# Moving elementwise work from GpSimd to VectorE, and reordering the convolution stage, in a two-layer hybrid trunk

## The chip, the cores and the metric

The kernel runs on one core of one Trainium2 chip, in one launch. The metric is the device time of one execution in microseconds. The engines are named as in the profile: PE is TensorE's matmul, PEld its weight load, DVE is VectorE, ACT is ScalarE, POOL is GpSimd and SP is SyncE, which issues most of the transfers. L508 is line 508 of the kernel's file.

## The reference

Two layers of a diffusion trunk run over 128 context tokens and 512 latent tokens with a width of 1024. Cut to what matters here:

```
mod = ada_w-projection of silu(condition)             # 6 vectors a layer: shift, scale, gate (twice)
h   = rmsnorm(x) * norm_w * (1 + scale) + shift
# layer 0
p   = h @ ab_w_in                  # DeltaNet q, k, v, gate z, a, b; attention q, k, v
qkv = silu(depthwise_conv5(dq, dk, dv));  dq, dk = l2norm(dq), l2norm(dk)
o_dn = rmsnorm(delta_forward(...) + delta_backward(...)) * silu(z)     # chunkwise, a triangular inverse a chunk
o_at = attention(rope(rmsnorm(aq)), rope(rmsnorm(ak)), av)
x   = x + gate * (concat(o_dn, o_at) @ ab_w_out);  x = x + gate * swiglu(adaln_norm(x))
# layer 1: the same frame with a bidirectional mLSTM as the mixer
```

All of it is float32. A product is made of three passes over two-part operands: each operand is split into a rounded part `hi` (fp32r) and the remainder `lo = x - hi`, and the products are hi·hi, lo·hi and hi·lo.

## The kernel before

Activations lie transposed, as 8 tiles of 128 features by 640 tokens. Weights come in a fixed order (`wspecs`); `WStream.fetch` loads a unit on the SP queue, casts `hi` on ScalarE (L483) and subtracts `lo` (L484) on the engine held in `W.eng`, up to three units ahead of the product that uses them. SBUF is handed out from 30 slots in the order in which they were freed. The framework orders each engine's instructions by program order and readiness; each engine then runs its own queue strictly in turn.

The stages that the change touches, in order:

- **Start** (`ada_start`). For each of 8 feature tiles: a scale vector from two VectorE reductions over a weight tile, then `nm.scale` (hi and lo of the scaled x) and `nm.square` (running sum of squares), and products of the first 272 output columns. For odd tiles lo and the running sum are made on GpSimd.
- **Convolutions** (`conv`, 12 feature tiles of k, q, v). A product of 48 matmuls (`qkv`), an evacuation to `cbuf`, one ScalarE and four VectorE taps (`cy`, L980), then a queue `later` of closures. `tick()` runs one closure after each product. The closure of tile n does its SiLU (L984), some modulation pieces (`ada_fill`, two VectorE reductions of 1024 columns, L323), and `then()`: five transposes on TensorE (`flip`, L992 and L994) and what follows them. So the transposes of tile n stand behind the product of tile n+1. The first two tiles use the scaled, not yet normalized x (`nm.raw`, the norm is applied in the evacuation as `cu`), while `nm.finish` makes the normalized `h` for the others.
- **Gate, attention queries and keys** (`gemm_tok` with `ev_z`, `ev_q`, `ev_kv`). Modulation pieces are attached to the evacuations: `ADA_CONV` gives 9 pieces to the convolutions, `ADA_Z` and `ADA_Q` 5 each, `ADA_KV` none. In `ev_q` the piece comes before the norm and rope of the tile.
- **Decay matrices** (L1157 to L1168): 40 VectorE products `up`, which read PSUM, followed by attention, and beside attention a triangular inversion on GpSimd (L1218, L1220) and then the DeltaNet scan.
- **Output projection of layer 0** (`out_half`, 16 units of 24 matmuls). Each unit is added into x by VectorE (`resid`, L558); in the second half the scale and the sum of squares of the next norm follow. The weight remainders and the sums of squares are GpSimd's.
- **Head of layer 1.** Four products with raw x, `nm.finish`, and then the token-major products. The weight remainders, and the scaling of the first two query tiles, are GpSimd's.

GpSimd has the powers for every reciprocal square root (`rsqrt`, L154) and its own DMA queue too.

Of the kernel before, what the change touches and what calls it, by code (L numbers as in the profile page):

```python
# [53 lines left out]
ADA_CONV, ADA_Z, ADA_Q, ADA_KV = [1] * 9 + [0] * 3, [1] * 5, [1] * 5, [0, 0, 0, 0, 0]  # L54
# [31 lines left out]
def tile_trunk(ctx: ExitStack, tc: tile.TileContext, A, dbg=None, stop=None):  # L86
# [101 lines left out]
    class Norm:  # L188
# [24 lines left out]
        def scale(self, k, x, eng=dve):  # L213
            h, sc = self.raw, self.sc
            v = None if eng is dve else t_tile("nv")[:, :T]
            for s, (a, b) in enumerate(SEG):
                act.activation((h.hi[k] if v is None else v)[:, a:b], x[:, a:b], AF.Copy, scale=sc(s, k))  # L217
                if v is None:
                    dve.scalar_tensor_tensor(out=h.lo[k][:, a:b], in0=x[:, a:b], scalar=sc(s, k),
                                             in1=h.hi[k][:, a:b].bitcast(F32), op0=ALU.mult, op1=ALU.subtract)  # L220
# [4 lines left out]
        def add(self, k, x, eng=dve):  # L225
            if self.raw:
                self.scale(k, x)
            self.square(k, x, eng)

        def square(self, k, x, eng=dve):  # L230
# [126 lines left out]
    def ada_start(nm):  # L357
# [15 lines left out]
        def x_in(k):  # L373
            sp.dma_start(out=xs[k], in_=A["x"][k])
            nm.square(k, xs[k], pool if k in (1, 3, 5, 7) else dve)
# [16 lines left out]
        def products(k):  # L392
# [3 lines left out]
            for t in range(NT):  # L396
# [6 lines left out]
              "s": lambda k: nm.scale(k, xs[k], pool if k in (1, 3, 5, 7) else dve)}  # L403
# [61 lines left out]
    class WStream:  # L465
        def __init__(self):
            self.i = 0
            self.eng = dve
# [92 lines left out]
    def out_half(mx, xs, l, half, nm, js=range(NK), fill=0, eng=dve, spill=None):  # L561

        for j in js:
            w = W.next(3)
            ps = g_tile("op")
            gemm_f(ps, w, mx, 4 * half, 4)
            U.put(*w[2])
            resid(ps, xs[j], mod[l][2], j)
            ada_fill(fill[j] if fill else 0, xs[j][:, 0:1])
            if nm is not None:  # L570
                nm.add(j, xs[j], eng)
            if spill is not None:
                pool.dma_start(out=spill[j], in_=xs[j])
# [285 lines left out]
    def layer0(nm, accs, ws, xt, xs):  # L859
        with ExitStack() as lay:  # L860
# [73 lines left out]
            def bias_b():  # L934
                for s in range(2):
                    pb = m_tile("shb")
                    pe.matmul(pb[:, :272], lhsT=ident[0:2, s:s + 1].to_broadcast([2, P]), rhs=shr[0:2, :272],
                              start=True, stop=True)
                    act.copy(shw[:, 272 * s:272 * s + 272], pb[:, :272])
                for t, n, b in ((slice(0, 1), 1, 0), (slice(1, NT), NT - 1, 272)):  # L940
                    pool.tensor_tensor(out=gat[:, t, :], in0=gat[:, t, :],
                                       in1=shw[:, None, b:b + 16].to_broadcast([P, n, 16]), op=ALU.add)
                    pool.tensor_tensor(out=zv[0][:, t, :], in0=zv[0][:, t, :],
                                       in1=shw[:, None, b + 16:b + 272].to_broadcast([P, n, 256]), op=ALU.add)
                act.activation(zv[0], zv[0], AF.Silu)
                gates_a()
# [13 lines left out]
            def conv(ft, x, out, then):  # L960
# [13 lines left out]
                tick()  # L974
# [28 lines left out]
            def after_k(hh):  # L1003
# [8 lines left out]
                if hh == 3:  # L1012
                    dve.tensor_scalar(out=ssk, in0=ssk, scalar1=EPS, scalar2=None, op0=ALU.add)
                    rsqrt(rk, ssk)
                    pool.tensor_tensor(out=nk, in0=ssk, in1=rk, op=ALU.mult)
                    pool.tensor_tensor(out=rk2, in0=rk, in1=rk, op=ALU.mult)
                    for d in range(2):
                        pool.tensor_tensor(out=bU[:, :, 4 * d:4 * d + 4], in0=beta[:, :, 4 * d:4 * d + 4], in1=rk2, op=ALU.mult)
                    pool.tensor_tensor(out=sK, in0=sK, in1=bU, op=ALU.mult)

            def after_q(hh):
                p0, p1 = flip(kq[hh][:, 648:1296])
                sumsq(ssq, hh, p0, p1)
                if hh == 3:
                    dve.tensor_scalar(out=ssq, in0=ssq, scalar1=EPS, scalar2=None, op0=ALU.add)
                    rsqrt(rq, ssq)
                    pool.tensor_scalar(out=rq, in0=rq, scalar1=128.0 ** -0.5, scalar2=None, op0=ALU.mult)
                    pool.tensor_tensor(out=rq2, in0=rq, in1=rq, op=ALU.mult)

            rk = sm([NT, 4], "rk")  # L1030
            W.eng = pool
# [4 lines left out]
            for hh in range(4):  # L1036
# [5 lines left out]
                if hh == 1:  # L1042
# [21 lines left out]
            W.eng = dve  # L1064
# [59 lines left out]
            def ev_kv(t, ps):  # L1124
                raw = t_tile("ak")
                act.copy(raw[:, :256], ps[:, 0:256])
                ada_fill(ADA_KV[t], raw[:, 0:1])
                act.copy(vav[:, t], v3(ps[:, 256:512], 2))
                n = norm_rope(t, raw, 2, kw)
                if t == 0:  # L1130
# [285 lines left out]
            def finish(c):  # L1416
# [9 lines left out]
                pool.tensor_tensor(out=rs, in0=rs, in1=rq[:, c, :], op=ALU.mult)  # L1426
# [58 lines left out]
    def layer1(nm, xt, xs, xd):  # L1485
        with ExitStack() as lay:
# [23 lines left out]
            W.eng = pool  # L1510
# [7 lines left out]
            for j in range(4):  # L1518
# [3 lines left out]
                (pool if j < 2 else dve).tensor_tensor(out=y[:, :T], in0=src[:, :T], in1=nm.bc[:, :T], op=ALU.mult)  # L1522
                for i in range(2):
                    r = slice(64 * i, 64 * i + 64)
                    for s, (a, b) in enumerate(SEG):
                        if j < 2:
                            pool.tensor_scalar(out=qp[2 * j + i][r, a:b], in0=y[r, a:b], scalar1=0.125,
                                               scalar2=bias[r, 2 * j + s:2 * j + s + 1], op0=ALU.mult, op1=ALU.add)
                        else:
                            act.activation(qp[2 * j + i][r, a:b], y[r, a:b], AF.Identity, scale=0.125,  # L1530
                                           bias=bias[r, 2 * j + s:2 * j + s + 1])
            nm.raw.put()
            U.put(nm.bc)
            W.eng = dve
# [376 lines left out]
    W.eng = dve  # L1911
# [8 lines left out]
    W.eng = pool  # L1920
# [4 lines left out]
    out_half(mx, xs, 0, 0, nm, fill=(1, 0, 0, 0, 0, 0, 0, 0), eng=pool, spill=xf)  # L1925
# [3 lines left out]
    W.eng = dve  # L1929
# [139 lines left out]
```

## Time and profile before

| what | us |
|---|---|
| three runs | 1732.96, 1734.18 (median), 1734.88 |
| the profiled execution, its own time | 1727.01 |
| its span, first to last instruction | 1725.1 |
| PE busy in the span | 1642.7 (95%) |
| DVE busy | 1242.5 (72%) |
| ACT busy | 764.4 (44%) |
| POOL busy | 268.4 (16%) |

The mean granted TensorE clock is 0.989 of full speed. Busy shares are averages over stages with different limits, so each stage that the change touches is to be read by itself.

### The profile page before, as it was taken

To read this page: it belongs to the slowest core of one execution; us is meant where nothing else is said; L and a number is where in the kernel's file an instruction comes from. 1 tells how busy PE (TensorE), PEld (TensorE's weight loads), DVE (VectorE), ACT (ScalarE), POOL (GpSimd) and SP (SyncE) were. 2 spreads that over 40 slices of the span, in tenths; PEclk is the share of its full clock that TensorE was granted. 3 is DMA by queue.
4 is the path that set the end of the run, shared out by engine and by line. 5 is a ranking of instruction groups with operands and counts; after the bars stand their busy time and mean duration, and the time that the engine had idled before them with its cause. 6 is when DMAs were issued, how large, how long until landed. Compare 5 with 4: busy or idle time off the path is not lost. (4 is left out here: it accounts for less than half of the span.)

```text
span 1725.1 us, 28119 instructions
## 1 busy us (share of the span) xinstructions
PE 1642.7 (95%) x10896; PEld 1565.6 (91%) x10896; DVE 1242.5 (72%) x2286; ACT 764.4 (44%) x1644; POOL 268.4 (16%) x318
## 2 busy tenths in 40 slices
PE   6888988998899999999999899999999999999998
PEld 3788876798899999999999889988999999999998
DVE  7798678778778889879755847457777988856432
ACT  5674256456364444442224423246455544434310
POOL 3344022663440000000002300001010000000000
PEclk9999999999999999999999999999999999999999
DMA  8233421104621444447633315411160344319321
GB/s 330 95 111 101 123 80 29 29 8 139 231 103 48 145 161 150 161 151 300 217 94 125 128 55 177 146 64 50 37 221 24 121 153 150 128 57 330 109 73 63
DMA packets 80653, 216.21 MB, mean 125 GB/s; under 512 B 20196, under 2 KB 21348, under 8 KB 80520
## 3 DMA queue, kind: packets, MB, share of 16 engines
q1 hardware_dynamic: 75720, 194.75, 34.0%
q0 software_dynamic: 4800, 19.66, 2.9%
q8 instruction: 86, 1.41, 0.3%
q14 instruction: 47, 0.39, 0.1%
HBM read 186.85 MB, written 27.53 MB: 124 GB/s over the span
## 5 line engine op out<-in xcount | busy, mean ns | idle before, releaser
L483 ACT CAST wh<-wr 128x1024 fp32r<-128x1024 f32 (+4 forms) x148 | 134.7, 914 | 296.2 <-DMA wr<-in_w_d 131.5
L508 PE MATMUL fd<-hid,wh 128*128 128x320 f32 x1408 | 264.4, 309 | 0.0
L508 PEld LDWEIGHTS fd<-hid,wh 128*128 128x128 f32 x1408 | 220.9, 188 | 0.3 <-ACT wh L483 0.3
L696 PE MATMUL sb<-ht,ph 128*128 128x320 f32 x1008 | 201.0, 313 | 3.8 <-DVE c L713 3.1
L484 DVE TENSOR_TENSOR wl<-wr,wh 128x1024 fp32r<-128x1024 f32 (+3 forms) x97 | 111.9, 1158 | 89.2 <-ACT wh L483 69.0
L696 PEld LDWEIGHTS sb<-ht,ph 128*128 128x128 f32 x1008 | 162.1, 190 | 6.6 <-DVE c L713 3.7
L508 PE MATMUL fd<-hid,wl 128*128 128x320 f32 x704 | 160.1, 309 | 1.4 <-DVE wl L484 1.4
L323 DVE SCALAR_TENSOR_TENSOR aj<-ar,cs 128x1024 bf16<-128x1024 f32 x112 | 133.6, 1219 | 24.4 <-DMA ar<-in_ada_w 24.2
L696 PE MATMUL sad<-hb,ph 128*128 128x320 f32 x576 | 128.4, 310 | 0.5 <-ACT sp L711 0.5
L508 PEld LDWEIGHTS fd<-hid,wl 128*128 128x128 f32 x704 | 117.9, 188 | 1.6 <-DVE wl L484 1.6
L508 PE MATMUL op<-mxh,wh 128*128 128x320 f32 x512 | 100.4, 314 | 7.3 <-DVE xb L558 5.1
L558 DVE SCALAR_TENSOR_TENSOR xd<-fd,mod,xd 128x128 f32<-128x128 f32 x96 | 48.4, 546 | 68.7 <-PE fd L508 68.6
L696 PEld LDWEIGHTS sad<-hb,ph 128*128 128x128 f32 x576 | 96.4, 188 | 1.1 <-ACT sp L711 1.1
L656 DVE TENSOR_TENSOR pl<-s,ph 128x1024 fp32r<-128x1024 f32 x72 | 88.0, 1222 | 4.1 <-ACT ph L655 3.6
L508 PEld LDWEIGHTS op<-mxh,wh 128*128 128x128 f32 x512 | 81.9, 191 | 8.7 <-ACT rh L217 5.3
L696 PE MATMUL sad<-hb,pl 128*128 128x320 f32 x288 | 89.0, 309 | 0.0
L696 PE MATMUL sb<-ht,pl 128*128 128x320 f32 x288 | 89.0, 309 | 0.0
L655 ACT CAST ph<-s 128x1024 fp32r<-128x1024 f32 x72 | 75.2, 1048 | 28.2 <-PE sad L696 9.2
L655 ACT CAST ph<-wp 128x1024 fp32r<-128x1024 f32 (+1 forms) x72 | 60.1, 835 | 41.4 <-PE sad L696 22.8
L824 POOL DMA_DIRECT2D hd<-c x18 | 9.8, 542 | 418.6 <-DVE c L823 418.6
L696 PE MATMUL sad<-ht,ph 128*128 128x320 f32 x288 | 64.9, 312 | 1.6 <-DVE c L707 1.4
L656 DVE TENSOR_TENSOR pl<-wp,ph 128x1024 fp32r<-128x1024 f32 x36 | 43.9, 1221 | 29.1 <-issue 21.1
(559 smaller groups left out, 4203.1 us busy)
## 6 DMA issues: line engine op xcount, KB each, us to landing
ar<-in_ada_w SPq DMA_DIRECT2D x61, 512.0 KB
wp<-in_w_g SPq DMA_DIRECT2D x36, 512.0 KB
wp<-in_w_u SPq DMA_DIRECT2D x36, 512.0 KB
wr<-in_w_d SPq DMA_DIRECT2D x32, 512.0 KB
hf<-hd SPq DMA_DIRECT2D x44, 320.0 KB
hd<-c POOLq DMA_DIRECT2D x36, 320.0 KB, 2.6
adas<-in_ada_w SPq DMA_DIRECT2D x19, 512.0 KB
wr<-in_w_ml SPq DMA_DIRECT2D x20, 416.0 KB
```

The lines of the kernel that those rows point to most:

```text
L323: dve.scalar_tensor_tensor(out=junk, in0=st, scalar=one, in1=ada["cs"][:, s, :], op0=ALU.mult, op1=ALU.mult, accum_out=mod[l][q][:, s, j:j ...
L483: act.copy(hi, raw[:, :n])
L484: self.eng.tensor_tensor(out=lo, in0=raw[:, :n], in1=hi.bitcast(F32), op=ALU.subtract)
L508: pe.matmul(ps[:, LO + a:LO + b], lhsT=wv[:, k, :], rhs=xk[:, a:b], start=k == 0 and p_ == 0, stop=k == kk - 1 and p_ == 2)
L558: dve.scalar_tensor_tensor(out=x[:, a:b], in0=ps[:, LO + a:LO + b], scalar=gate[:, s, j:j + 1], in1=x[:, a:b], op0=ALU.mult, op1=ALU.add)
L655: act.copy(hi, src)
L656: dve.tensor_tensor(out=lo, in0=src, in1=hi.bitcast(F32), op=ALU.subtract)
L696: pe.matmul(bank[o], lhsT=wv[:, k, :], rhs=xv, start=o not in seen and k == 0 and p_ == 0, stop=k == 3 and p_ == 2, skip_group_check=True)
L824: pool.dma_start(out=hd[f], in_=c1)
```

## The change

SBUF arithmetic of GpSimd goes to VectorE: the remainders of weights, the odd tiles' lo parts and sums of squares, two additions of a bias, some small products, and two query tiles of layer 1 (whose last step goes to ScalarE). The reciprocal square roots' powers, the inversion and some memsets stay on GpSimd. In the convolutions `tick(2)` runs two closures after a product and `then` is queued again instead of called, so that the transposes of tile n stand behind the product of tile n+2. The third tile uses the raw x as well. Five modulation pieces leave the convolutions for the keys' evacuations, and the queries' pieces move behind their norm and rope.

```diff
-ADA_CONV, ADA_Z, ADA_Q, ADA_KV = [1] * 9 + [0] * 3, [1] * 5, [1] * 5, [0, 0, 0, 0, 0]
+ADA_CONV, ADA_Z, ADA_Q, ADA_KV = [0] * 4 + [1, 0] * 4, [1] * 5, [1] * 5, [1] * 5
@@ Norm.scale
-            v = None if eng is dve else t_tile("nv")[:, :T]
             for s, (a, b) in enumerate(SEG):
-                act.activation((h.hi[k] if v is None else v)[:, a:b], x[:, a:b], AF.Copy, scale=sc(s, k))
-                if v is None:
-                    dve.scalar_tensor_tensor(out=h.lo[k][:, a:b], ...)
-            if v is not None:
-                act.copy(h.hi[k][:, :T], v)
-                eng.tensor_tensor(out=h.lo[k][:, :T], in0=v, in1=h.hi[k][:, :T].bitcast(F32), op=ALU.subtract)
+                act.activation(h.hi[k][:, a:b], x[:, a:b], AF.Copy, scale=sc(s, k))
+                dve.scalar_tensor_tensor(out=h.lo[k][:, a:b], ...)
@@ Norm.square
-                eng.tensor_tensor(out=self.acc, in0=self.acc, in1=sq, op=ALU.add)
+                dve.tensor_tensor(out=self.acc, in0=self.acc, in1=sq, op=ALU.add)
@@ WStream.fetch
-                self.eng.tensor_tensor(out=lo, in0=raw[:, :n], in1=hi.bitcast(F32), op=ALU.subtract)
+                dve.tensor_tensor(out=lo, in0=raw[:, :n], in1=hi.bitcast(F32), op=ALU.subtract)
@@ bias_b, twice
-                    pool.tensor_tensor(out=zv[0][:, t, :], ...)
+                    dve.tensor_tensor(out=zv[0][:, t, :], ...)
@@ conv
-                tick()
+                tick(2)
@@ rest, in conv
-                    then()
+                    later.append(then)
@@ the four key tiles
-                if hh == 1:
+                if hh == 2:
                     x.put()
@@ ev_q (ev_kv alike)
-                ada_fill(ADA_Q[t], raw[:, 0:1])
                 n = norm_rope(t, raw, 4, qw)
+                ada_fill(ADA_Q[t], n[:, 0:1])
@@ layer1
-                (pool if j < 2 else dve).tensor_tensor(out=y[:, :T], in0=src[:, :T], in1=nm.bc[:, :T], op=ALU.mult)
+                dve.tensor_tensor(out=y[:, :T], in0=src[:, :T], in1=nm.bc[:, :T], op=ALU.mult)
...
-                        if j < 2:
-                            pool.tensor_scalar(out=qp[2 * j + i][r, a:b], ...)
-                        else:
-                            act.activation(qp[2 * j + i][r, a:b], ...)
+                        act.activation(qp[2 * j + i][r, a:b], ...)
```

## Rows read from the trace of the kernel before

**Rows 1.** The page's part on engines: busy us (share of the span) xinstructions.

```profile
PE 1642.7 (95%) x10896; PEld 1565.6 (91%) x10896; DVE 1242.5 (72%) x2286; ACT 764.4 (44%) x1644; POOL 268.4 (16%) x318
```

**Rows 2.** Busy time by stage: stretch, length, busy per engine, clock, DMA share, GB/s.

```profile
0.00:59.09 59.09, 44.60 (x212) 25.99 (x213) 41.83 (x63) 34.36 (x65) 19.14 (x18) 1.00 0.71 268
59.09:176.36 117.27, 100.07 (x638) 97.28 (x637) 106.86 (x177) 73.11 (x181) 48.38 (x25) 0.93 0.30 101
220.00:283.76 63.76, 52.10 (x297) 42.61 (x295) 51.62 (x157) 40.05 (x149) 12.50 (x11) 0.97 0.16 51
430.00:480.00 50.00, 44.26 (x290) 43.80 (x289) 38.87 (x69) 17.77 (x27) 23.32 (x19) 0.97 0.64 216
943.00:990.00 47.00, 41.68 (x249) 40.20 (x249) 37.55 (x58) 19.70 (x34) 17.39 (x19) 0.93 0.35 116
```

**Rows 3.** TensorE's waits over the whole span: us in total, times, longest.

```profile
PE tr L992 <- ACT kq L984: 12.3, 4, 6.3
...
PE op L508 <- DVE xb L558: 5.1, 1, 5.1
PE qkv L508 <- ACT hh L269: 4.9, 1, 4.9
PE tkm L545 <- POOL v L1541: 4.0, 1, 4.0
...
PE ot L1438 <- DVE of L1432: 3.3, 3, 1.9
PE tka L399 <- POOL rl L223: 3.2, 3, 1.1
```

**Rows 4.** VectorE's timeline in the convolutions: start, us, instruction.

```profile
93.69 1.28 DVE L323 SCALAR_TENSOR_TENSOR adaj<-adas,one,cs 128x1024 bf16<-128x1024 f32 x1
...
95.01 3.31 DVE L323 SCALAR_TENSOR_TENSOR adaj<-adas,one,cs 128x1024 bf16<-128x1024 f32 x1
...
98.25 3.02 DVE L980 SCALAR_TENSOR_TENSOR cy<-cbuf,cw,cy 128x644 f32<-128x644 f32 x1
...
104.28 0.89 DVE L980 SCALAR_TENSOR_TENSOR cy<-cbuf,cw,cy 128x644 f32<-128x644 f32 x1
...
128.84 0.89 DVE L980 SCALAR_TENSOR_TENSOR cy<-cbuf,cw,cy 128x644 f32<-128x644 f32 x1
```

**Rows 5.** GpSimd's timeline in the same stage.

```profile
94.66 5.92 POOL L484 TENSOR_TENSOR wl<-wr,wh 128x1024 fp32r<-128x1024 f32 x2 [20.08 <-ACT wh L483]
...
126.95 4.19 POOL L154 TENSOR_TENSOR rk<-ssk,mhalf 128x20 f32<-128x20 f32 x1 [5.79 <-DVE one L336]
```

**Rows 6.** VectorE's groups by shape, 56 to 180 us: count, busy, mean ns, idle before.

```profile
L980 DVE SCALAR_TENSOR_TENSOR cy<-cbuf,cw,cy 128x644 f32<-128x644 f32 x45 | 54.5, 1217 | 4.5 <-ACT cy L978 4.1
L323 DVE SCALAR_TENSOR_TENSOR adaj<-adas,one,cs 128x1024 bf16<-128x1024 f32 x18 | 27.3, 1517 | 0.3
...
L484 DVE TENSOR_TENSOR wl<-wr,wh 128x1024 fp32r<-128x1024 f32 x3 | 3.7, 1226 | 0.1
```

**Rows 7.** GpSimd's groups over the whole span.

```profile
L484 POOL TENSOR_TENSOR wl<-wr,wh 128x1024 fp32r<-128x1024 f32 (+1 forms) x19 | 49.8, 2634 | 72.0 <-ACT wh L483 59.7 <-DVE nu L267 8.2 <-PE fd L508 4.2
...
L237 POOL TENSOR_TENSOR nacc<-nacc,nsq 128x640 f32<-128x640 f32 x11 | 21.7, 1973 | 16.8 <-ACT nsq L236 15.8 <-DVE rl L219 1.0
L484 POOL TENSOR_TENSOR wh<-wr,wh 128x512 fp32r<-128x512 f32 x15 | 20.8, 1400 | 32.8 <-ACT wh L483 32.8
```

**Rows 8.** TensorE's timeline behind the wait of 4.27 us at 118.4.

```profile
123.69 0.73 PE L508 MATMUL qkv<-hh,wh 128*128 128x320 f32 x2
...
126.74 0.46 PE L508 MATMUL qkv<-hh,wh 128*128 128x320 f32 x2
```

**Rows 9.** Busy time by stretch around the keys, columns as in rows 2.

```profile
250.00:260.00 10.00, 9.81 (x62) 8.47 (x61) 4.85 (x18) 6.89 (x28) 2.79 (x4) 1.00 0.08 25
260.00:270.00 10.00, 8.74 (x70) 8.06 (x71) 9.31 (x36) 7.79 (x32) 1.81 (x3) 1.00 0.00 1
```

**Rows 10.** VectorE's remainders of half-width weight units over the whole span, as rows 6.

```profile
L484 DVE TENSOR_TENSOR wh<-wr,wh 128x512 fp32r<-128x512 f32 x17 | 11.7, 688 | 6.6 <-ACT wh L483 6.6
```

More of the change, by code (lines that the diff above doesn't have):

```diff
@@ L211, in shift, with scale, add, square @@
                 dve.tensor_tensor(out=lo, in0=sh[:, 2 * i:2 * i + 2], in1=hi.bitcast(F32), op=ALU.subtract)
-        def scale(self, k, x, eng=dve):
+        def scale(self, k, x):
             h, sc = self.raw, self.sc
-            v = None if eng is dve else t_tile("nv")[:, :T]
             for s, (a, b) in enumerate(SEG):
-                act.activation((h.hi[k] if v is None else v)[:, a:b], x[:, a:b], AF.Copy, scale=sc(s, k))
-                if v is None:
-                    dve.scalar_tensor_tensor(out=h.lo[k][:, a:b], in0=x[:, a:b], scalar=sc(s, k),
-                                             in1=h.hi[k][:, a:b].bitcast(F32), op0=ALU.mult, op1=ALU.subtract)
-            if v is not None:
-                act.copy(h.hi[k][:, :T], v)
-                eng.tensor_tensor(out=h.lo[k][:, :T], in0=v, in1=h.hi[k][:, :T].bitcast(F32), op=ALU.subtract)
-        def add(self, k, x, eng=dve):
+                act.activation(h.hi[k][:, a:b], x[:, a:b], AF.Copy, scale=sc(s, k))
+                dve.scalar_tensor_tensor(out=h.lo[k][:, a:b], in0=x[:, a:b], scalar=sc(s, k),
+                                         in1=h.hi[k][:, a:b].bitcast(F32), op0=ALU.mult, op1=ALU.subtract)
+        def add(self, k, x):
             if self.raw:
                 self.scale(k, x)
-            self.square(k, x, eng)
-        def square(self, k, x, eng=dve):
+            self.square(k, x)
+        def square(self, k, x):
             if self.acc is None:
@@ L374, in x_in @@
             sp.dma_start(out=xs[k], in_=A["x"][k])
-            nm.square(k, xs[k], pool if k in (1, 3, 5, 7) else dve)
+            nm.square(k, xs[k])
         def sc_in(k):
@@ L402, in ada_start @@
         do = {"w": sc_in, "x": x_in, "n": sh_in, "W": W.fetch, "t": products,
-              "s": lambda k: nm.scale(k, xs[k], pool if k in (1, 3, 5, 7) else dve)}
+              "s": lambda k: nm.scale(k, xs[k])}
         stats = nm.stats()
@@ L559, in resid, with out_half @@
                                      in1=x[:, a:b], op0=ALU.mult, op1=ALU.add)
-    def out_half(mx, xs, l, half, nm, js=range(NK), fill=0, eng=dve, spill=None):
+    def out_half(mx, xs, l, half, nm, js=range(NK), fill=0, spill=None):
         for j in js:
@@ L570, in out_half @@
             if nm is not None:
-                nm.add(j, xs[j], eng)
+                nm.add(j, xs[j])
             if spill is not None:
@@ L1026, in after_q @@
                     rsqrt(rq, ssq)
-                    pool.tensor_scalar(out=rq, in0=rq, scalar1=128.0 ** -0.5, scalar2=None, op0=ALU.mult)
-                    pool.tensor_tensor(out=rq2, in0=rq, in1=rq, op=ALU.mult)
+                    dve.tensor_scalar(out=rq, in0=rq, scalar1=128.0 ** -0.5, scalar2=None, op0=ALU.mult)
+                    dve.tensor_tensor(out=rq2, in0=rq, in1=rq, op=ALU.mult)
             rk = sm([NT, 4], "rk")
-            W.eng = pool
             x = nm.raw
@@ L1126, in ev_kv @@
                 act.copy(raw[:, :256], ps[:, 0:256])
-                ada_fill(ADA_KV[t], raw[:, 0:1])
                 act.copy(vav[:, t], v3(ps[:, 256:512], 2))
                 n = norm_rope(t, raw, 2, kw)
+                ada_fill(ADA_KV[t], n[:, 0:1])
                 if t == 0:
@@ L1425, in finish @@
                 rsqrt(rs, so)
-                pool.tensor_tensor(out=rs, in0=rs, in1=rq[:, c, :], op=ALU.mult)
+                dve.tensor_tensor(out=rs, in0=rs, in1=rq[:, c, :], op=ALU.mult)
                 yield
@@ L1525, in layer1 @@
                     for s, (a, b) in enumerate(SEG):
-                        if j < 2:
-                            pool.tensor_scalar(out=qp[2 * j + i][r, a:b], in0=y[r, a:b], scalar1=0.125,
-                                               scalar2=bias[r, 2 * j + s:2 * j + s + 1], op0=ALU.mult, op1=ALU.add)
-                        else:
-                            act.activation(qp[2 * j + i][r, a:b], y[r, a:b], AF.Identity, scale=0.125,
-                                           bias=bias[r, 2 * j + s:2 * j + s + 1])
+                        act.activation(qp[2 * j + i][r, a:b], y[r, a:b], AF.Identity, scale=0.125,
+                                       bias=bias[r, 2 * j + s:2 * j + s + 1])
             nm.raw.put()
             U.put(nm.bc)
-            W.eng = dve
             gt = sm([NT, 32], "gt")
@@ L1924, in tile_trunk @@
     xd, xf = (dram.tile([NK, P, T], F32, name=n) for n in ("xd", "xf"))
-    out_half(mx, xs, 0, 0, nm, fill=(1, 0, 0, 0, 0, 0, 0, 0), eng=pool, spill=xf)
+    out_half(mx, xs, 0, 0, nm, fill=(1, 0, 0, 0, 0, 0, 0, 0), spill=xf)
     ada_fill(max(0, len(ada_todo) - 56))
```

18 lines of the change are left out of this document (6 added, 12 removed).

## The prediction

> **What bounds the kernel now.** I read the page's part on engines first: TensorE is busy 95% of the span [rows 1], so almost all time is its products, which the change leaves alone. Only what keeps TensorE waiting or slow can go. The second view is TensorE's list of waits [rows 3]. Its long entries lie where the change lies: 12.3 us before the convolutions' transposes, for the SiLU that feeds them; 4.9 before the fourth convolution, for the normalized h; 5.1 in layer 0's output projection, where the sum into x has not yet freed a PSUM buffer; 4.0 and 3.2 on remainders that GpSimd makes, in layer 1's head and the start; 3.3 on the normed DeltaNet output. The third view, busy time by stage, gives each stage's room [rows 2]: in the convolutions (59.09 to 176.36) TensorE is busy 100.07 of 117.27 us and VectorE 106.86, so VectorE is the fuller engine.
>
> Why is VectorE full? Its timeline shows it. A modulation half takes 1.28 us at 93.69 and the same instruction 3.31 us at 95.01; a convolution tap takes 3.02 at 98.25 and 0.89 at 104.28 [rows 4]. Meanwhile GpSimd runs two weight remainders from 94.66, in 5.92 us together [rows 5]. They interleave: GpSimd's first, VectorE's half, GpSimd's second, VectorE's tap, which ends about 0.7 us after GpSimd does. So the two engines take turns here: while GpSimd runs a two-input subtraction, a VectorE instruction with two SBUF inputs stands still. GpSimd's help costs VectorE about as long as GpSimd's instruction lasts, 2.4 us and more [rows 5], for a remainder that VectorE makes in 1.23 [rows 6].
>
> After a long wait TensorE is slower as well: behind the one that ends at 122.67 two matmuls show 0.73 us, at 126.74 they show 0.46 [rows 8]; the granted clock of the stage is 0.93 [rows 2].
>
> **The change, part by part.** Negative is time saved on TensorE's path. I make the sum against the profiled execution's own 1727.01 us, which lies 7.2 below the runs' median of 1734.18; the 7.2 is added at the end.
>
> *Convolutions.* Room: the waits are 117.27 - 100.07 = 17.2 us. The clock costs at most 0.07 x 117.27 = 8.2 more, and nothing if it was low only while TensorE idled, so the room is 17.2 to 25.4. I take 23, since rows 8 show slow matmuls behind the wait. What VectorE will carry: the taps' stretch is 45 x (1.217 - 0.89) = 14.7 us, the modulation halves' 18 x (1.517 - 1.28) = 4.3, together 19 [rows 4, 6]. Twelve remainders at 1.23 come in, 14.8, and some 2.5 for two bias additions and the third raw tile (an estimate from remainders of like width). Five pieces leave; a piece is two halves, 2.6, so 13 [rows 4]. That makes 106.86 - 19 + 17.3 - 13 = 92 us, about what TensorE needs with its room gone: 117.27 - 23 = 94. VectorE is no longer the fuller engine, but barely. The taps' delay matters less than before: a transpose used to stand right behind the product that follows its own, so the evacuation, five tap instructions and the SiLU had one product (94 / 12, some 7.8 us with its transposes) to finish, and the longest wait was 6.3 [rows 3]; now they have two. The wait of 4.9 for h goes the same way: h is wanted one product later, and its VectorE work is not held up. Queued behind a late transpose were all later products and, behind them, the evacuations; nothing takes that place while the taps keep up. One more raw tile holds its SBUF slots a product longer; weights are fetched three units ahead, which covers a transfer that starts one product late (7.8 us if it does not). Ends: -25 if TensorE runs through; -12 if VectorE's 92 us become some 105 because its queue also waits for ScalarE and TensorE (it idles 10.4 of 117.27 now). I take -20, nearer to the first, since the transposes have a product to spare.
>
> Here a rule can be weighed. GpSimd keeps its powers for the square roots, one of 4.19 us in this stage [rows 5], and during it VectorE's tap at 128.84 took 0.89 as usual [rows 4]. So what stays on GpSimd here costs VectorE nothing, and the sum has nothing for it. The Trainium skill (page "SBUF — State Buffer", section "SBUF: two separate sides") says that the port pair shared by the two engines is locked exclusively for a whole instruction and that the loser fully blocks. For the subtractions the trace agrees, 3.31 against 1.28. For the power it does not: by the rule this 4.19 us and its twin for the queries would go on holding VectorE, and the convolutions would give some 8 us less, -12.
>
> *Gate, queries and keys.* The 5 pieces, 13 us, now enter VectorE's queue at the keys' norms, ahead of the 40 decay products and, behind them, the first score reductions. Cover: VectorE is busy 4.85 of the 10 us from 250 and 9.31 of the next ten [rows 9], which leaves 5.8 us. TensorE is busy 52.10 of 63.76 there [rows 2], so it already waits and a delay reaches it. Ends: 0 (the queries' transposes come earlier, since the pieces stand behind their norm, and the keys' pieces fill VectorE's waits for GpSimd's powers), and +13 (no cover, all in front). 13 - 5.8 = 7.2; part is given back by the queries, so I take +5.
>
> *Output projection of layer 0.* Waits 5.1 + 3.3, and 0.03 x 50 = 1.5 of clock: room 10 [rows 2, 3]. VectorE's sum into x was late because GpSimd was at 15 remainders and 7 of the 11 sums of squares of [rows 7]. On VectorE these are 15 x 0.69 = 10.4 [rows 10] and 7 x 0.8 (between 0.69 for 512 columns and 0.89 for 644: an estimate) = 5.6, spread over 16 units; the stage now has 38.87 of 50 on VectorE [rows 2], part of it the same stretch. Ends: -10 and 0 (in the second half sum, scale, square and remainder make VectorE the bound). I take -7.
>
> *Head of layer 1.* The wait of 4.0 is for a remainder that GpSimd made while VectorE held it off: it idled 8.2 us behind VectorE's norm [rows 7]. With 0.07 x 47 = 3.3 for the clock [rows 2] the room is 7. On VectorE the remainder stands in the norm's queue, and two multiplications come in; two tiles' scaling goes to ScalarE, busy 19.70 of 47. Ends: -7 and +1 (one remainder of 1.23 late). I take -4.
>
> *Start.* Three waits of 3.2 us in all on GpSimd's lo parts [rows 3], and one ScalarE cast less for each odd tile. But transfers fill 0.71 of the stage [rows 2], and VectorE gets four sums and eight lo parts for the stretch it loses. Ends: -4 and +2. I take -2.
>
> Sum: -20 + 5 - 7 - 4 - 2 = -28. 1727.0 - 28 = 1699.0; with the 7.2, 1706.
>
> **The rivals.** *A: VectorE becomes the bound.* It takes all the remainders in turn. Convolutions -12, keys +10, projection -5, head -3, start -1: -11, 1723. For it: the 92 us against 94. Against: two products of slack for the taps.
>
> *B: everything hides.* Convolutions -25, keys 0, projection -10, head -5, start -3: -43, 1691. For it: VectorE's free time around 250. Against: the 40 decay products behind the pieces.
>
> *C, the other side: the stretch is not GpSimd's doing.* Then moved work is only added: 19 x 1.23 + 15 x 0.69 + 11 x 0.8 = 43 us more of VectorE [rows 6, 7, 10], and the slow instructions stay. The convolutions keep their length (17 in, 13 out, transposes later), and the work shows where VectorE has no room: keys +13, projection and head +5 together, +18, 1752. It decides from the point where less than some 18 us of the stage waits go. Against it: the slow instructions end just after GpSimd's, in the case read above. *D: GpSimd's powers hold VectorE up as its subtractions do.* The two of some 4.19 us in the convolutions then take back 8.4, which give -12, and the rest stays: -20, 1714 [rows 5]. Rows 4 speak against it. This is what the rule above would make of the powers.
>
> **How the numbers follow.** Forecast 0.55 (its own range 1697 to 1716, the convolutions between -16 and -24 the keys between +2 and +9, and 2 us for the small terms), A 0.18, B 0.13, C 0.07, D 0.07. The time is the forecast's, 1706. The range of 8 in 10 reaches to A and just to B: 1691 to 1725; outside are C, half of B and a little of A. About 0.2% (3.5 us) is what a measurement of this kernel can tell from no change. Faster by more: the forecast, B, D and nearly all of A, 0.90. Slower by more: C, with a little of A, 0.06. Within: 0.04.
>
> **What would show it.** In the changed kernel's convolutions no tap above 1 us and no modulation half above 1.4; TensorE's wait for the SiLU under 2 us in all; the stage from the first to the last convolution some 97 us long; the granted clock there near 1.00. Around the keys VectorE without gaps, the decay products some 5 us later relative to the last key product, and TensorE's waits there longer. In the projection no wait of 5 us. The prediction is wrong if taps of 3 us remain (C), if VectorE runs through the convolutions without a gap while TensorE waits (A), or if weights arrive late because slots are held longer.

## The result, and the profile after

The changed kernel takes 1710.45 us (median of 4 runs, 1707.9 to 1712.19), the kernel before 1734.23 beside it: a ratio of 0.9863, 95% interval 0.9846 to 0.988. That is 23.8 us less. Between the two profiled executions it is 17.5 us (1727.01 against 1709.51), since the profiled execution of before was a low one.

The page's part on engines, changed kernel, as [rows 1]:

```profile
PE 1638.0 (96%) x10896; PEld 1563.9 (92%) x10896; DVE 1229.6 (72%) x2359; ACT 763.0 (45%) x1646; POOL 153.4 (9%) x243
```

GpSimd lost 115 us of busy time and VectorE gained none: 1242.5 before, 1229.6 now, with 73 instructions more. So moved work replaced time in which VectorE had stood still. The busy time by stage, columns as in [rows 2], the same five stages where they now lie:

```profile
0.00:56.47 56.47, 44.60 (x212) 25.94 (x213) 41.35 (x75) 31.88 (x61) 2.62 (x10) 1.00 0.75 280
56.47:152.40 95.93, 93.62 (x635) 92.32 (x634) 79.29 (x166) 69.78 (x179) 7.69 (x2) 0.98 0.28 89
196.00:277.00 81.00, 61.67 (x327) 50.27 (x326) 70.34 (x199) 42.76 (x160) 15.56 (x11) 0.92 0.29 84
417.00:467.00 50.00, 46.87 (x317) 46.11 (x316) 40.55 (x86) 20.68 (x39) 3.39 (x5) 1.00 0.68 236
925.10:972.00 46.90, 44.84 (x284) 44.16 (x283) 35.54 (x65) 26.64 (x46) 2.83 (x6) 1.00 0.38 122
```

The convolutions, 117.27 us before, last 95.93, with TensorE busy 93.62 of them and the clock at 0.98. VectorE's groups there, by shape, columns as in [rows 6]:

```profile
L974 DVE SCALAR_TENSOR_TENSOR cy<-cbuf,cw,cy 128x644 f32<-128x644 f32 x42 | 37.1, 888 | 5.9 <-ACT cy L972 5.4
L478 DVE TENSOR_TENSOR wl<-wr,wh 128x1024 fp32r<-128x1024 f32 x13 | 15.9, 1219 | 0.0
L318 DVE SCALAR_TENSOR_TENSOR adaj<-adas,one,cs 128x1024 bf16<-128x1024 f32 x6 | 7.7, 1283 | 0.1
```

A tap takes 0.89 us, not 1.22, and a modulation half 1.28, not 1.52. TensorE's waits over the whole span, as [rows 3]:

```profile
PE apt L1259 <- DVE pm L1251: 11.1, 4, 10.3
...
PE pv L1371 <- DVE rv L1357: 2.4, 1, 2.4
...
PE tr L986 <- ACT kq L978: 2.3, 1, 2.3
PE tkm L539 <- DVE wl L478: 2.1, 1, 2.1
...
PE op L502 <- DVE one L331: 1.8, 1, 1.8
```

The 12.3 us for the SiLU are 2.3 now, the 4.9 for h and the 5.1 in the projection are gone (short waits of 1.8 and 1.8 us in all are left there), the 4.0 in layer 1's head is 2.1. Three waits have grown by over 2 us: 10.3 us in the attention (`apt`), 2.4 in the scan (`pv`), and 3.1 in the feed-forward, for a weight's cast, in a stretch that got only 0.4 us longer. The first is not all new. The kernel before stood 5.9 us just ahead of its first `apt`, in front of the scores (`as`), and these two waits are gone or nearly gone:

```profile
PE as L1249 <- ACT pm L1255: 3.7, 1, 3.7
PE as L1249 <- ACT up L1165: 2.1, 1, 2.1
```

The next table is worked out from the start times of TensorE's instructions in the two traces: how long each stretch lasts, in us.

| stretch | before | after | difference | predicted |
|---|---|---|---|---|
| start, to the first `qkv` | 59.1 | 56.5 | -2.6 | -2 |
| to the last `qkv` (convolutions) | 117.0 | 95.5 | -21.5 | -20 |
| to the first `mq` (gate, queries, keys, attention) | 166.2 | 181.4 | +15.2 | +5 |
| to the first `op` (scan) | 80.1 | 82.8 | +2.7 | not in the sum |
| to the first `fg` (projection of layer 0) | 67.8 | 60.9 | -6.9 | -7 |
| to the first `mqk` (feed-forward) | 445.1 | 445.5 | +0.4 | 0 |
| to the first `num` (head of layer 1) | 200.0 | 194.4 | -5.6 | -4 |
| to the end of the span | 589.8 | 590.7 | +0.9 | 0 |

Where the 15.2 us came back is plain in the timeline. First TensorE, then VectorE, in the same stretch of the changed kernel:

```profile
260.83 0.39 PE L1242 MATMUL as<-ckt,qt 128*128 128x128 f32 x2
271.52 1.12 PE L1259 MATMUL apt<-cm,pm 128*128 128x128 f32 x4 [10.31 <-DVE pm L1251]
```

```profile
253.87 1.27 DVE L318 SCALAR_TENSOR_TENSOR adaj<-adas,one,cs 128x1024 bf16<-128x1024 f32 x1
...
255.33 1.27 DVE L318 SCALAR_TENSOR_TENSOR adaj<-adas,one,cs 128x1024 bf16<-128x1024 f32 x1
...
256.53 7.06 DVE L1160 SCALAR_TENSOR_TENSOR up<-kk,bU,up 128x128 f32<-128x128 f32 x27
263.51 4.18 DVE L1188 COPY uc<-up 32x160 f32<-32x160 f32 x16
267.72 0.69 DVE L1244 TENSOR_REDUCE smx<-as 128x4 f32<-128x512 f32 x1
```

The last of the keys' modulation halves ends at 256.6. Only then come 27 of the 40 decay products, 16 copies, and at 267.72 the first reduction of the scores, for which TensorE has stood since 261.2. Behind the wait TensorE is slow, in the windows of this stretch:

```profile
262.00:272.00 10.00, 0.48 (x2) 0.45 (x3) 9.54 (x35) 7.25 (x26) 0.00 (x0) 0.71 0.24 75
...
272.00:282.00 10.00, 10.00 (x55) 7.84 (x55) 5.62 (x17) 4.89 (x13) 4.07 (x11) 0.78 0.36 45
```

TensorE does next to nothing from 262 to 272, and in the next ten microseconds, with no wait, its granted clock is 0.78. The kernel before has such a stretch too, just behind its own first `apt` at 285.6, but a milder one:

```profile
286.00:296.00 10.00, 10.00 (x74) 8.66 (x73) 7.09 (x22) 5.63 (x14) 5.07 (x13) 0.95 0.19 29
```

So the clock costs there about 2 us more than before (10 x 0.17), an estimate from these two rows.

The scan's new wait is of another kind. VectorE's timeline, and TensorE's row that waits for it:

```profile
391.11 0.16 DVE L1418 TENSOR_TENSOR ors<-ors,rq 128x4 f32<-128x4 f32 x1 [1.01 <-POOL ors L154]
...
393.01 0.16 DVE L1418 TENSOR_TENSOR ors<-ors,rq 128x4 f32<-128x4 f32 x1 [1.00 <-POOL ors L154]
393.09 2.15 DVE L1357 SCALAR_TENSOR_TENSOR rv<-kqs,negegc,v 128x128 f32<-128x128 f32 x8
```

```profile
393.49 1.00 PE L1371 MATMUL pv<-rv,up 128*128 128x128 f32 x6 [2.35 <-DVE rv L1357]
```

A product of four columns, which GpSimd used to make right behind its own power, now stands in VectorE's queue. It takes 0.16 us, but VectorE stands 1.0 us for the power in front of it, and `rv` and other work of the scan stand behind it. VectorE's list of waits shows all of this kind that the change made (us in total, times, longest):

```profile
DVE ors L1418 <- POOL ors L154: 5.1, 5, 1.2
DVE rq L1021 <- POOL rq L154: 3.6, 1, 3.6
DVE nk L1009 <- POOL rk L154: 3.4, 1, 3.4
```

### The profile page after: what moved, and what is told of

Its sections match the earlier page's. It is cut to its first block, busy times and chain, and to the rows that moved or that the text cites. A ratio compares the mean times of both kernels' runs of the same rounds, so it can differ in the third digit from the quotient of the medians.

```text
span 1707.7 us, 28082 instructions
## 1 busy us (share of the span) xinstructions
PE 1638.0 (96%) x10896; PEld 1563.9 (92%) x10896; DVE 1229.6 (72%) x2359; ACT 763.0 (45%) x1646; POOL 153.4 (9%) x243
## 5 line engine op out<-in xcount | busy, mean ns | idle before, releaser
L478 DVE TENSOR_TENSOR wl<-wr,wh 128x1024 fp32r<-128x1024 f32 (+3 forms) x116 | 133.1, 1151 | 91.6 <-ACT wh L477 68.5
L650 DVE TENSOR_TENSOR pl<-wp,ph 128x1024 fp32r<-128x1024 f32 x36 | 43.9, 1220 | 29.5 <-issue 21.5
L690 PE MATMUL sb<-hn,ph 128*128 128x320 f32 x288 | 64.7, 309 | 0.0
```

Of the source, the lines that this page charges most:

```text
L478: dve.tensor_tensor(out=lo, in0=raw[:, :n], in1=hi.bitcast(F32), op=ALU.subtract)
L650: dve.tensor_tensor(out=lo, in0=src, in1=hi.bitcast(F32), op=ALU.subtract)
L690: pe.matmul(bank[o], lhsT=wv[:, k, :], rhs=xv, start=o not in seen and k == 0 and p_ == 0, stop=k == 3 and p_ == 2, skip_group_check=True)
```

## The experiments

Twelve kernels ran. All compute the whole reference. Each was timed against the kernel before; the medians of before beside them were 1732.42 (runs 1 to 4), 1733.24 (5 to 8) and 1731.54 (9 to 12), and 1734.23 beside the changed kernel. Differences between kernels of different groups are given by the medians; since before's own median moves by up to 2.7 us, they are good to some 3 us, and the ratios are the fairer comparison. Lengths of stages come from one profiled execution each.

### 1 to 4: which part of the change does what

**Run 1, the pieces back in the convolutions.**

```diff
-ADA_CONV, ADA_Z, ADA_Q, ADA_KV = [0] * 4 + [1, 0] * 4, [1] * 5, [1] * 5, [1] * 5
+ADA_CONV, ADA_Z, ADA_Q, ADA_KV = [1] * 9 + [0] * 3, [1] * 5, [1] * 5, [0, 0, 0, 0, 0]
```

> The changed kernel with the modulation pieces where they were (nine in the first nine convolutions, none at the keys); all else as changed. Theory (the five pieces at the keys stand in front of the decay products on VectorE, which runs there without a gap, so their 13 us reach TensorE's path nearly whole; VectorE has 16 us of room in the changed convolutions, 79.3 busy of 95.9): the inversion's first product comes 9 to 13 us earlier after the last conv product, the convolutions lose 0 to 4, the time is 1698 to 1702. Rival (the pieces are covered, and what came back around the keys is due to the transposes that lie two products later or to the queries' pieces behind their norm): the convolutions lose 0 to 4, nothing is gained at the keys, 1710 to 1714.

1706.54 us, ratio 0.9858 (0.9844 to 0.9873): between the two. The convolutions lost 4.8 us of their gain (last `qkv` at 156.8, not 152.0); from there to the first `mq` it is 171.2 us, 10.2 less than the changed kernel's 181.4. So the pieces at the keys do cost some 10 us, but back in the convolutions they cost half of that. Why VectorE, with 16 us free by my count, could not take them was open.

**Run 2, the engines alone.** GpSimd's arithmetic on VectorE as in the change; order and pieces as before (run 1's line too).

```diff
-                tick(2)
+                tick()
...
-                    later.append(then)
+                    then()
...
-                if hh == 2:
+                if hh == 1:
                     x.put()
...
+                ada_fill(ADA_Q[t], raw[:, 0:1])
                 n = norm_rope(t, raw, 4, qw)
-                ada_fill(ADA_Q[t], n[:, 0:1])
```

> The kernel before with GpSimd's arithmetic on VectorE everywhere, and nothing else of the change: transposes one product later, two raw tiles, pieces and their order as before. Theory (GpSimd's subtractions and VectorE's two-input SBUF instructions take turns): no tap above 1 us, VectorE busy some 93 to 97 us in the convolutions instead of 107, convolutions 12 to 18 us shorter, start, projection and head of layer 1 together 13 to 16 shorter, nothing given back at the keys: 1701 to 1709. Rival C of the prediction (moved work is only added): convolutions at least as long as before, 1740 to 1752. Second rival (the order makes the gain in the convolutions, the engines little): convolutions 0 to 5 shorter, 1714 to 1721.

1704.69 us, ratio 0.985 (0.9833 to 0.9866): 5.8 us below the whole change by the medians, some 2 by the ratios, whose intervals overlap. So at the least the rest of the change adds nothing to it. No tap is above 1 us:

```profile
L974 DVE SCALAR_TENSOR_TENSOR cy<-cbuf,cw,cy 128x644 f32<-128x644 f32 x44 | 38.3, 885 | 0.1
```

Rival C of the prediction falls here: moved work was not added. The convolutions are 15.3 us shorter (101.7 from the first to the last `qkv`), and the keys give nothing back (first `apt` 17.5 earlier than before, last `qkv` 17.9).

**Run 3, the order alone.** The other half: GpSimd keeps its arithmetic; transposes, raw tile and pieces as in the change (run 2's lines the other way round, on the kernel before).

> The kernel before with the order of the change alone: transposes two products later, third raw tile, pieces to the keys, queries' pieces behind the norm; GpSimd keeps its arithmetic. Theory: stretched taps of 3 us remain, but five pieces fewer and a product more of slack take 8 to 14 us out of the convolutions, the keys give 11 to 15 back, nothing changes elsewhere: 1731 to 1740. Rival (the order alone makes the whole gain of the convolutions, 20 or more): 1723 to 1729.

1734.05 us, ratio 1.0015 (1.0 to 1.0029). As the theory had it: the convolutions 11.9 us shorter (105.1), and from the last `qkv` to the first `mq` 13.7 longer (179.9). The order is worth nothing by itself.

**Run 4, the convolutions' weight remainders back on GpSimd.**

```diff
             rk = sm([NT, 4], "rk")
+            W.eng = pool
...
                 conv(8 + hh, h, y, lambda hh=hh, y=y: after_v(hh, y))
+            W.eng = dve
```

> The changed kernel with the weight remainders of the convolution stage alone back on GpSimd. Theory (taking turns): taps of up to 3 us come back, VectorE's busy time in the stage does not fall by the 14 to 17 us of remainders that leave it but stays at 79 to 95, and TensorE loses 0 to 6 us, since the transposes have two products of slack: 1710 to 1716. Rival (GpSimd runs beside VectorE): VectorE falls to some 63 to 66 us busy, no tap above 1 us, time equal or up to 3 us less than the changed kernel: 1707 to 1710.

1727.01 us, ratio 0.9977 (0.9964 to 0.999): 16.6 us above the changed kernel, where I expected 0 to 6. These twelve instructions alone take back two thirds of the change or more. The convolutions take 107.4 us from the first to the last `qkv`, 11.9 more; the other 4.8 are lost between there and the first `mq` (186.2 us against 181.4) and were not followed up. The stage's window, TensorE's longest wait in the stage, and then the timelines of VectorE, ScalarE and GpSimd:

```profile
56.50:164.30 107.80, 96.79 (x633) 94.65 (x631) 84.92 (x147) 67.42 (x176) 38.69 (x14) 0.94 0.24 79
```

```profile
113.95 0.48 PE L987 MATMUL tr<-cm,kq 128*128 128x128 f32 x1 [7.11 <-ACT kq L979]
```

```profile
97.30 7.72 DVE L975 SCALAR_TENSOR_TENSOR cy<-cbuf,cw,cy 128x644 f32<-128x644 f32 x4 [1.51 <-ACT cy L973]
...
105.23 2.12 DVE L906 TENSOR_SCALAR ngc<-gc 128x40 f32<-128x40 f32 x1
107.26 2.40 DVE L907 TENSOR_TENSOR sK<-glb,gc 128x40 f32<-128x40 f32 x1
```

```profile
109.69 0.24 ACT L910 ACTIVATE sK<-sK 128x40 f32<-128x40 f32 x1 [4.10 <-DVE sK L907]
```

```profile
98.28 11.32 POOL L479 TENSOR_TENSOR wl<-wr,wh 128x1024 fp32r<-128x1024 f32 x4 [4.13 <-ACT wh L478]
```

VectorE's busy time did not fall by the remainders that left it (15.9 us); it rose from 79.29 to 84.92 in a longer stage. Four GpSimd remainders in a row hold four taps (7.72 us for 3.6), and then two instructions of 40 columns, which take 0.2 us otherwise and 2.12 and 2.40 here. The taps lose some 4 us, and the two short instructions another 4. The first I had expected; what I had missed is the second: a short instruction in a chain becomes about as long as GpSimd's. ScalarE waits 4.10 us for `sK`, its SiLU stands behind that, and TensorE waits 7.11.

By the Trainium skill (page "SBUF — State Buffer", section "SBUF: two separate sides") the loser of the shared ports is blocked for the other's whole instruction. The trace agrees for these subtractions: two instructions of 0.2 us took 2.12 and 2.40 beside remainders of 2.3 to 3.1.

### 5 to 8: VectorE behind GpSimd's powers, and the projection

**Runs 5 and 6, the small products behind the powers back on GpSimd** (the five behind the keys' power, of which one is shown, the two behind the queries', and the one in the scan), in the changed kernel (5) and in run 2's kernel (6).

```diff
                     rsqrt(rk, ssk)
-                    dve.tensor_tensor(out=nk, in0=ssk, in1=rk, op=ALU.mult)
+                    pool.tensor_tensor(out=nk, in0=ssk, in1=rk, op=ALU.mult)
...
                     rsqrt(rq, ssq)
-                    dve.tensor_scalar(out=rq, in0=rq, ...)
-                    dve.tensor_tensor(out=rq2, in0=rq, in1=rq, op=ALU.mult)
+                    pool.tensor_scalar(out=rq, in0=rq, ...)
+                    pool.tensor_tensor(out=rq2, in0=rq, in1=rq, op=ALU.mult)
...
                 rsqrt(rs, so)
-                dve.tensor_tensor(out=rs, in0=rs, in1=rq[:, c, :], op=ALU.mult)
+                pool.tensor_tensor(out=rs, in0=rs, in1=rq[:, c, :], op=ALU.mult)
```

> The changed kernel with only the small products that follow GpSimd's powers back on GpSimd (five after the keys' power, two after the queries', one after each power of the scan's output norm). Theory (VectorE takes its queue strictly in turn, so a 0.16 us product moved behind a power makes VectorE stand for the power: 3.4, 3.6 and five times 1.0 us, and all that is queued behind stands too): the scan's wait of 2.4 us for rv is gone, the scan's end comes 2 to 4 us earlier after the last mq, the convolutions change by 0 to -2, the time is 1704 to 1708. Rival (these waits are covered by VectorE's room): 1709 to 1712, and the wait for rv stays or moves to another tile.

> The kernel before with its order and pieces kept, and GpSimd's arithmetic on VectorE but for the small products behind the powers, which stay on GpSimd. Theory: 2 to 4 us less in the scan than with all arithmetic moved (1704.7), and 1 to 4 less in the convolutions, where VectorE had 91 of 102 us to carry and stood 5.6 us behind the powers: 1697 to 1702, and so faster than both kernels of the case. Rival (the waits are covered): 1703 to 1706.

Run 5: 1706.05 us, 4.4 below the changed kernel (ratio 0.9844, 0.9826 to 0.9861, which overlaps the changed kernel's; the traces have to tell). Its wait for `rv` is back at what it was before, on TensorE's timeline:

```profile
390.88 1.00 PE L1371 MATMUL pv<-rv,up 128*128 128x128 f32 x6 [0.26 <-DVE rv L1357]
```

From the last `mq` to the first `op` it takes 21.0 us against the changed kernel's 25.4 and the 22.6 of before. Its convolutions are as long as the changed kernel's (95.5).

Run 6: 1694.63 us, ratio 0.9776 (0.9761 to 0.979), 10.1 below run 2 and 15.8 below the changed kernel. Its convolutions took 96.0 us against run 2's 101.7. In run 2 VectorE had stood 3.42 and 2.22 us behind the two powers, 5.6 together, about what the stage gained (5.7):

```profile
120.05 0.18 DVE L1009 TENSOR_TENSOR nk<-ssk,rk 128x20 f32<-128x20 f32 x1 [3.42 <-POOL rk L154]
...
145.98 0.18 DVE L1021 TENSOR_SCALAR rq<-rq 128x20 f32<-128x20 f32 x1 [2.22 <-POOL rq L154]
```

In run 6 the same power runs beside VectorE, which goes on at its usual pace. GpSimd's timeline, then VectorE's:

```profile
117.48 4.50 POOL L154 TENSOR_TENSOR rk<-ssk,mhalf 128x20 f32<-128x20 f32 x1 [64.96 <-DVE ssk L1007]
```

```profile
118.51 1.24 DVE L478 TENSOR_TENSOR wl<-wr,wh 128x1024 fp32r<-128x1024 f32 x1
119.68 1.27 DVE L318 SCALAR_TENSOR_TENSOR adaj<-adas,one,cs 128x1024 bf16<-128x1024 f32 x1
...
120.88 0.88 DVE L974 SCALAR_TENSOR_TENSOR cy<-cbuf,cw,cy 128x644 f32<-128x644 f32 x1
```

So the 16 us of room that I counted in the changed convolutions held 7 us in which VectorE stood behind the powers (3.4 and 3.6). With those waits gone, the nine pieces fit: run 9, which is run 1 with the small products on GpSimd, takes 95.8 us for the convolutions, where run 1 took 100.3.

**Run 7, the keys' pieces at the last gate tile, small products on GpSimd.**

```diff
-ADA_CONV, ADA_Z, ADA_Q, ADA_KV = [0] * 4 + [1, 0] * 4, [1] * 5, [1] * 5, [1] * 5
+ADA_CONV, ADA_Z, ADA_Q, ADA_KV = [0] * 4 + [1, 0] * 4, [1, 1, 1, 1, 6], [1] * 5, [0] * 5
```

> The changed kernel with the keys' five modulation pieces attached to the last gate tile instead (six pieces there), where VectorE was busy 1.5 of 10 us behind them, and the small products behind the powers on GpSimd. Theory (a piece costs nothing where VectorE is idle and 13 us in front of the decay products): the convolutions keep their 24 us, the attention's first transposed products come 22 to 24 us earlier than before, not 14, the scan loses under 2: 1692 to 1698. Rival (the transposes that lie two products later give back at the keys what they gain, whatever the pieces do): 14 to 17 us at the attention, 1700 to 1705.

1699.7 us, ratio 0.9803 (0.9789 to 0.9818), between the theory's range and the rival's. VectorE took the pieces where it had been idle, but everything behind them in its queue came later, a weight remainder of the queries too, for which TensorE waits at 214 us:

```profile
PE tka L539 <- DVE wl L478: 3.4, 1, 3.4
```

The first `apt` is 19.9 us earlier than before, not 22 to 24 (the theory) or 14 to 17 (the rival). Idle time of VectorE ahead of the need was not free either.

**Run 8, the projection of layer 0 on GpSimd again.**

```diff
     ada_open()
+    W.eng = pool
     out_half(mx, xs, 0, 1, None, ...)
...
-    out_half(mx, xs, 0, 0, nm, ..., spill=xf)
+    out_half(mx, xs, 0, 0, nm, ..., eng=pool, spill=xf)
...
     mx.put()
+    W.eng = dve
```

> The changed kernel with the output projection of layer 0 alone as before: weight remainders and the sums of squares of its second half on GpSimd. Theory (the projection gained 7 us of its own): the stretch from its first product to the first product of the feed-forward gets 5 to 9 us longer, a wait of some 5 us for the sum into x comes back, 1715 to 1719. Rival (GpSimd's help there was free, and the gain came from the earlier start): unchanged within 2 us, 1708 to 1712.

1722.45 us, ratio 0.9939 (0.9924 to 0.9954): 12.0 above the changed kernel. The projection itself is 6.7 us longer (67.6), with its old wait:

```profile
PE op L503 <- DVE xb L553: 5.0, 1, 5.0
```

The other 5 to 6 us are lost ahead of it: the first `op` is 5.6 us later than in the changed kernel, at least in part because the projection's first remainders are made during the scan: beside two of them VectorE's product behind the power takes 1.23 us, not 0.16, and the eight `of` instructions 3.19, not 2.18.

### 9 to 12: from the fastest kernel, one part at a time

Run 6 is the base of these four.

**Run 9, the order of the change with the old pieces** (transposes two later, third raw tile, queries' pieces behind the norm: run 2's lines the other way round). **Run 10, only the transposes two later.**

> The changed kernel with the small products behind the powers on GpSimd and the modulation pieces in the first nine convolutions: it differs from the fastest so far (arithmetic on VectorE, those small products on GpSimd, old order, 1694.6) by the order alone: transposes two products later, third raw tile, queries' pieces behind their norm. Theory (the order gives nothing once VectorE no longer stands behind the powers, since TensorE's waits for the SiLU are nearly gone either way): 1693 to 1698. Rival (the order itself costs what comes back around the keys): 1701 to 1706.

> The fastest kernel so far with the transposes two products later and nothing else. Theory: the convolutions gain 0 to 3 us, the gate gets the last transposes and loses 0 to 2: 1692 to 1697. Rival (the two products of slack matter by themselves): the convolutions gain 4 or more and keep it, 1687 to 1691.

Run 9: 1696.55 us, 0.9797 (0.9781 to 0.9813). Run 10: 1691.91, 0.9782 (0.9758 to 0.9806). Neither can be told from run 6 by its ratio, and the convolutions take 95.8 and 95.2 us against 96.0. Run 10 may be the fastest of all by a little; with these intervals that stays open.

**Run 11, the pieces where the change puts them.** Run 1's line, the other way round.

> The fastest kernel so far with the pieces where the change puts them (four in the convolutions, five at the keys). Theory (in front of the decay products the pieces reach TensorE's path with 8 to 12 of their 13 us; in the convolutions their absence gives 0 to 4 us): 1699 to 1706, and TensorE's wait for the attention's first normalized row is some 10 us long again. Rival (the wait at the attention came from the transposes two products later): 1692 to 1696.

1706.6 us, ratio 0.9856 (0.9842 to 0.9871): 12.0 above run 6 and just above the theory's range. The convolutions are the same (96.1), so the absence of five pieces gave them nothing. VectorE is full around the keys and TensorE waits at the attention. Two windows and TensorE's row:

```profile
250.00:260.00 10.00, 8.42 (x54) 6.48 (x52) 10.00 (x33) 6.19 (x23) 1.11 (x2) 1.00 0.19 55
260.00:270.00 10.00, 0.00 (x0) 0.00 (x0) 9.72 (x33) 6.38 (x23) 0.00 (x0) 0.73 0.14 51
```

```profile
270.86 1.11 PE L1259 MATMUL apt<-cm,pm 128*128 128x128 f32 x4 [11.11 <-DVE pm L1251]
```

The first `apt` is 6.3 us later than in run 6 (270.9 against 264.6), the first `mq` 9.7 (332.5 against 322.8), the first `op` 11.7 (413.0 against 401.3). So the pieces cost about 6 where they stand, and the rest is added behind them. TensorE's clock does not add it: it is as low behind the first `apt` of run 6 as behind run 11's (run 6 first).

```profile
264.60:274.60 10.00, 10.00 (x62) 8.97 (x60) 5.62 (x18) 5.55 (x14) 4.61 (x12) 0.79 0.25 37
```

```profile
270.90:280.90 10.00, 10.00 (x56) 7.70 (x57) 6.16 (x19) 5.13 (x13) 3.79 (x11) 0.80 0.33 48
```

The delay also takes a second way. The input of GpSimd's inversion is copied out behind the decay products, so the inversion starts 7.2 us later (276.3 against 269.1); it lasts 38.8 and 38.9 us, and the first `mq` needs its result.

**Run 12, the head of layer 1 on GpSimd again** (remainders, and the scaling of two query tiles, as in the kernel before).

> The fastest kernel so far with the head of layer 1 as before: its weight remainders and the scaling of two query tiles on GpSimd. Theory (this term of the change gains by itself): the head, from its first product to the first product of the mLSTM's numerators, gets 4 to 7 us longer, a wait of some 4 us for a remainder of GpSimd comes back: 1699 to 1702. Rival (covered): 1693 to 1696.

1699.3 us, ratio 0.9812 (0.9797 to 0.9828): 4.7 above run 6. The head is 4.2 us longer (200.8 against 196.6, first `mqk` to first `num`), and the old wait is there:

```profile
PE tkm L540 <- POOL v L1534: 4.2, 1, 4.2
```

## Why the prediction was right, and where it was not

The time came out 4 us above the forecast of 1706, well inside its range. The sum behind it was 10.6 us too good (-28 against -17.4 between the two traces), and the offset made up for most of that: I added 7.2 us, by which the profiled execution of before lay under its median, as if that belonged to the kernel. The changed kernel's profiled execution lies 0.9 under its own median. So 6.3 us of the agreement is an accident of one low execution.

- **GpSimd and VectorE take turns: right**, and the root of the gain. The engines alone give 27.7 us (run 2); twelve remainders put back cost 16.6 (run 4). Taps of 0.89 and halves of 1.28 are as forecast, and so are the stage's 95.5 us (some 97) and its clock of 0.98; the 2.3 us for the SiLU just miss (under 2). Rival C, its opposite, fell.
- **Convolutions, -20: the size right (-21.5), the reason half right.** I gave the credit to VectorE's lighter load and to the transposes' second product. With the order and pieces of before, and the small products left on GpSimd, the stage gains as much: 21.0 us (run 6, 96.0 against 117.0). With GpSimd's arithmetic in place, the new order and the five pieces' leaving give 11.9 us together (run 3). Once the arithmetic has moved, they earn something only against waits that the change itself put in, and the pieces earn most of it: with VectorE standing behind the powers, the stage takes 101.7 us in the old order (run 2), 100.3 in the new order with the old pieces (run 1), and 95.5 with the five pieces gone as well (the changed kernel).
- **"So what stays on GpSimd here costs VectorE nothing": the step that failed by omission.** It holds for the ports: in run 6 VectorE kept its pace beside a power of 4.50 us, and rival D in its wording fell. But I costed the small products that move as arithmetic and did not ask what they stand behind. In VectorE's queue each one makes VectorE wait for a power: 3.4, 3.6 and five times 1.0 us. The scan, which was not in the sum at all, got 2.7 us longer; with these products alone put back it is 4.3 shorter (run 5, 78.5 against 82.8). Putting them back gave 4.4 us in the changed kernel, which the ratios alone do not tell from noise, and 10.1 in run 2's, which they do.
- **Keys, +5: the mis-sized term**, measured +15.2. "13 - 5.8 = 7.2" is near what the pieces cost at the place where they stand (6.3 us at the first `apt`, run 11). Two things were wrong around it. The queries gave back under 1 us: the changed kernel's lead over before is 22.1 us at the first of their transposes and 22.6 at the last. And I stopped at the first wait. Behind it the delay grows, to 9.7 us at the first `mq` and 11.7 at the end of the scan (run 11). VectorE and GpSimd's inversion, which starts 7.2 us late, are nearly full through the attention (VectorE 7.9 to 8.6, GpSimd 8.7 to 9.0 of each 10 us from 282 to 312) and catch nothing up. What adds the last 4 or 5 us is not shown. Runs 9 and 11 together show that the pieces, not the transposes, are the main cause: with the whole order but the old pieces, the stretch from the last `qkv` to the first `mq` is 169.1 us long (run 9), 11.8 less than run 5's 180.9, which differs by the pieces alone. The remaining 3 us of the 15.2 (run 9's 169.1 against the 166.2 of before) have another cause, which was not looked for.
- **Projection, -7: right**, -6.9, and by the reason given (run 8: +6.7 and the old wait).
- **Head of layer 1, -4: near**, -5.6; undone in run 12 it costs 4.2. Kernels with the changed head took 194.4 to 196.7 us there and those with the old one 200.0 to 201.4, so one pair of executions is good to some 2 us.
- **Start, -2:** -2.6, but this term can't be told from chance. Kernels with the same start reached the first `qkv` at 56.5 us in some profiled executions and at 58.1 to 58.3 in others, and with the old start at 59.1 and 62.2 (run 3).
- **Rival A** (VectorE becomes the bound, 1723) fell in the convolutions, where in run 6 VectorE carried 91.31 of 96.40 us while TensorE ran nearly through, and came true at the keys alone. My 92 us for VectorE was 79.29: one more piece slid past the stage's end, two taps too, and other two-input work had been stretched as well. **Rival B** (everything hides, 1691) is nearly what run 10 reaches with other placing.

What stays open: whether the transposes' second product is worth 1 to 3 us, and where the pieces lie best. They were not tried one by one.

## What to carry to other kernels

Before work is split between GpSimd and VectorE, see in the timeline whether the one's instruction stretches the other's; if it does, the split can cost more than it saves, most of all where a chain of short instructions stands beside the long one. When such work is moved back, leave with GpSimd small products that consume GpSimd's own results, since the consumer drags its wait into the new engine's queue. And price work that is put in front of a chain at everything behind it, not at the first wait: free time earlier in the queue covers it only if the work can start then.

## What was not expected of the hardware

Beside GpSimd's weight remainders VectorE instructions of 40 columns took 2.12 and 2.40 us instead of about 0.2 (run 4), one of them with a single tensor input. Beside a power of 4.50 us of 20 columns VectorE's two-input instructions kept their 0.88 to 1.27 us (run 6). So what GpSimd computes, and on how much, decides whether VectorE stands still. Run 6 hints at the size: right behind that power GpSimd makes products of two SBUF inputs, as the subtractions are, on 20 and 40 columns, and four taps beside them take 3.33 us together, no longer than usual (GpSimd, then VectorE):

```profile
123.03 1.49 POOL L1012 TENSOR_TENSOR bU<-beta,rk 128x20 f32<-128x20 f32 x2
```

```profile
122.72 3.33 DVE L974 SCALAR_TENSOR_TENSOR cy<-cbuf,cw,cy 128x644 f32<-128x644 f32 x4
```

A power on as many columns as a weight remainder has was not run, so it is not shown that the operation plays no part.
